# Expert stage of a hybrid encoder block: transposes gathered into long stretches, a third gather buffer and a second one-hot set

## Chip, core and metric

The kernel runs on one NeuronCore of a Trainium2 chip. The metric is the device time of one execution in microseconds (us), given as the median of the runs shown. A core has a matrix engine (TensorE, PE in the profile), a vector engine (DVE), a scalar engine (ACT), GpSimd (POOL) and SyncE (SP); the last two issue most of the DMAs. Matrix products land in PSUM, which has eight banks of 128 x 512 float32.

## The reference, cut to what matters

One encoder layer on 512 tokens of width 1024: attention and a state-space mixer, then a mixture of 16 experts in 4 groups, of which each token takes two. The change lies in the expert part alone. The reference computes every expert on every token and weighs it:

```
for e in range(N_EXPERTS):
    y_e = (jax.nn.silu(t @ w1[e]) * (t @ w3[e])) @ w2[e]
    out = out + combine[:, e:e + 1] * y_e
```

w1 and w3 are 1024 x 512, w2 is 512 x 1024, all float32: 6 MB for an expert, 96 MB for the 16.

## The kernel before

Each expert has 96 slots for its tokens. The 16 experts are taken in four **quads**: quad q holds the experts 4j + q, j = 0 to 3, one for each strip of 32 columns of the TensorE array. A **row block** r (0 to 2) of a quad is 128 rows: 32 slots of each of its four experts. For each of the 12 pairs (q, r) the kernel does this:

- **One-hot and indices.** `s_oh` writes on DVE which token sits in which slot (bf16, 128 x 512), `s_mm` multiplies it on TensorE (banks `pia`, `piq`) with the table `rc`, which holds token numbers and weights, and `s_ix` turns the result into indices.
- **Gather.** `gather` is an indirect DMA of GpSimd that fetches 128 tokens of 1024 float32 from `h2_d` into a gather buffer (`GS`). Row block (0, 0) comes without a gather.
- **Turn.** `t_mm` transposes the tokens on TensorE, four 128 x 128 blocks to a PSUM bank `pg`, two banks for a row block; `t_out` copies them to `TH`, on ACT (first half) and DVE (second).
- **Up.** `up_mm` multiplies with w1 (bank `pu`) and w3 (`pv`): eight jobs of four matmuls, each in a strip of 32 columns, that run side by side. `g_silu` and `g_mul` make the gated product in `s_buf`.
- **Turn again.** `s_t` transposes the product into one bank `ps`, and `s_out` copies it.
- **Down.** `down_mm` multiplies with w2 (bank `py`, two halves h, four k each), `y_ev` scales the result into `YS`.
- **Scatter.** An indirect DMA of GpSimd adds the 128 rows to `out`. Each scatter waits for the one before it, since both add to the same tensor.

The quads are interleaved in 12 phases, `u` (w1), `v` (w3) and `w` (w2): u0 v0 u1 w0 v1 u2 w1 v2 u3 w2 v3 w3. In quad 0, row block 0 goes through u and v first, then blocks 1 and 2. Each float32 matmul leaves two records in the trace, so that a job of up or down shows as eight. In w3 the order is row block by row block, so that block 0 needs the last weights of all, its k = 3, after a few jobs; the three last scatters then follow one another.

The **weights** come in 192 loads of 512 KB, 16 to a phase, issued by SP in the order of use. A load needs a free buffer of the pool "e". There are 35: 18 of their own, 3 that staged earlier weights, and 14 that come free as earlier tiles die, two from each call of `more` (tiles `EXm`, `EXx0`, `EXx1`, `EXr0`, `EXr1`, `EXu0`, `EXu1`). A buffer is free again when all row blocks have used it (`spent`).

The order on TensorE, ACT, DVE and GpSimd is laid down when the program is built: `Plan.run` is a list scheduler over jobs with costs, dependences, buffer pools and priorities (`prio`). Each engine then runs its list in that order.

Of the kernel before, what the change touches and what calls it, by code (L numbers as in the profile page):

```python
# [214 lines left out]
def tile_block(ctx: ExitStack, tc: tile.TileContext, x, norm_mix_w, w_in, b_gate, q_norm_w, k_norm_w,  # L215
# [19 lines left out]
    def bank(tag, nm):  # L235
        return psp.tile([P, 512], F32, tag=tag, name=nm, bufs=PSB[tag])
# [1349 lines left out]
    ohp = [cp.tile([P, NT, P], BF16, name="oh_%d" % i) for i in range(NR)]  # L1586

# [7 lines left out]
    def T_(q, r):  # L1595
        i = (q % 2) * NR + r
        return TH[i // 2][:, i % 2]

    def g_buf(R):
        return GS[0][:, R % NG, :]  # L1600

    def y_buf(r):
        return YS[r][:, :]
# [1 line left out]
    def s_buf(r):  # L1605
        return (YS[3][:, 0:512], YS[3][:, 512:1024], GS[1][:, 0, 0:512])[r]

    def sT_(r):
        return (GS[1][:, 0, 512:1024], GS[1][:, 1, 0:512], GS[1][:, 1, 512:1024])[r].rearrange(K4, k=4)

    def rooms():
        for t in TH + GS:
            t[:, 0]
        for t in YS:
            t[:, 0:512]


    def s_oh(q, r):
        V.tensor_tensor(ohp[r].rearrange("p t (j i) -> p t j i", j=4),
                        iota[:, r * RN:(r + 1) * RN].unsqueeze(1).unsqueeze(1).to_broadcast([P, NT, 4, RN]),  # L1620
                        slot.rearrange("p t (j q) -> p t j q", q=NQ)[:, :, :, q:q + 1].to_broadcast([P, NT, 4, RN]),
                        op=ALU.is_equal)

    def s_mm(nm, q, rs, n):
        t_["pi", nm] = bank("tp", "pi" + nm)
        for r in rs:
            for t in range(NT):
                T.matmul(t_["pi", nm][:, r * 18:r * 18 + n], lhsT=ohp[r][:, t, :], rhs=rc[:, t, q, 0:n], start=(t == 0),
                         stop=(t == NT - 1))

    def pi_(nm):
# [25 lines left out]
    def gather(g, i):  # L1657
        G.indirect_dma_start(g, None, h2_d, bass.IndirectOffsetOnAxis(ap=i, axis=0))

    def t_mm(q, r, kb):  # L1660
        g = g_buf(NR * q + r)
        pt = t_["pg", q, r, kb] = bank("tp", "pg%d_%d_%d" % (q, r, kb))
        for j in range(4):
            T.transpose(pt[:, j * P:(j + 1) * P], g[:, (kb * 4 + j) * P:(kb * 4 + j + 1) * P], ident)  # L1664

    def t_out(q, r, kb, src):
        o, i = T_(q, r)[:, kb * 4:kb * 4 + 4, :], src.rearrange(K4, k=4)
        if kb:
# [39 lines left out]
    def s_t(q, r):  # L1708
        t_["ps", q, r] = bank("tp", "ps%d_%d" % (q, r))
        for j in range(4):  # L1710
            T.transpose(t_["ps", q, r][:, j * P:(j + 1) * P], s_buf(r)[:, j * P:(j + 1) * P], ident)  # L1711

    def s_out(q, r):
        A.activation(sT_(r), t_["ps", q, r].rearrange(K4, k=4), AF.Copy)  # L1714
# [34 lines left out]
    jw, jT, jti, jsT, jy, jmul, jgx = {}, {}, {}, {}, {}, {}, {}  # L1749
    for x_, q in phases:  # L1750
        for kk in range(4):
            for j in range(4):
# [3 lines left out]
                    [j_rq] + ([last["e"]] if "e" in last else []), ["e"], prio=1000 + len(jw), lat=DLAT)  # L1756

    def sl_jobs(q):
        o = (0, at["u", 0] + 60, at["u", 1] - 90, at["u", 2] - 90)[q] or 700
        rs = list(range(NR))  # L1760
        oh = [job("dve", 0.6, lambda r=r: s_oh(q, r), [j_slot[t] for t in range(NT)] + (jti.get(q - 1, [])[:1]),
                  prio=o + (0 if r else 15) * (q == 0)) for r in rs]
# [23 lines left out]
    def t_jobs(q):
        for r in range(NR):
            o = (1900, at["v", 0] + 40 + 6 * r) [q] if q < 2 else at["w", q - 2] + 1 + r if r < 2 else at["v", q - 1] + 3
            jT[q, r] = []
            for kb in range(2):  # L1790
                tk = ["T"] * (kb == 0)
                if (q, r) == (0, 0):
                    k_, free = pgj[kb], ["sc"]
                else:
                    k_ = [job("pe", 0.55, lambda r=r, kb=kb: t_mm(q, r, kb), [jgx[q, r]] + jT[q, r], ["tp"],
                              ["G"] if kb else [], prio=o + r, duty=0.5)]
                    free = ["tp"]
                jT[q, r] = jT[q, r] + [job(
                    "dve" if kb else "act", 0.6 if kb else 0.48,
                    lambda r=r, kb=kb: t_out(q, r, kb, t_["pg", kb] if (q, r) == (0, 0) else t_["pg", q, r, kb]),  # L1800
                    k_ + [j_rooms], tk, free, prio=o - 1500)]

    def up_jobs(x_, q, prev, rs=tuple(range(NR))):
        o, tags = at[x_, q] + 30 * (q == 0 and rs[0] > 0), ("sc", "sc", "sc") if x_ == "v" else ("mm", "mm", "ac")
        nk = KD
        order_ = [(r, k) for k in range(nk) for r in rs]
        if (x_, q) == ("v", NQ - 1):
            order_.sort(key=lambda o_: o_ if o_[1] >= nk - 2 else (-1, o_[1]))
        for n, (r, k) in enumerate(order_):
            dep = [jw[x_, q, k // 2, j] for j in range(4)] + jT[q, r] + prev  # L1810
            end = (r, k % 2) == (NR - 1, 1)

            def f(r=r, k=k, end=end):
# [166 lines left out]
```

## Time and profile before

| | us |
|---|---|
| median of 3 runs | 670.3 (668.96 to 670.93) |
| the profiled execution, its own time | 669.12 |
| its span in the profile | 667.3 |
| TensorE busy in it | 645.5 |

The expert stage is the stretch from about 380 us to the end. "Busy" of TensorE counts any instruction in flight, so a full share says that it always had work, not that all of this work is needed. Load and landing times are those of the profile; a transfer's landing is the time at which its semaphore tells of it. Weights are moved by DMA queue q1, gathers and scatters by GpSimd's queue q0, and all of them by the same 16 DMA engines.

### The profile page before, as it was taken

To read this page: it belongs to the slowest core of one execution; us is meant where nothing else is said; L and a number is where in the kernel's file an instruction comes from. 1 tells how busy PE (TensorE), PEld (TensorE's weight loads), DVE (VectorE), ACT (ScalarE), POOL (GpSimd) and SP (SyncE) were. 2 spreads that over 40 slices of the span, in tenths; PEclk is the share of its full clock that TensorE was granted. 3 is DMA by queue.
4 is the path that set the end of the run, shared out by engine and by line. 5 is a ranking of instruction groups with operands and counts; after the bars stand their busy time and mean duration, and the time that the engine had idled before them with its cause. 6 is when DMAs were issued, how large, how long until landed. Compare 5 with 4: busy or idle time off the path is not lost. (4 is left out here: it accounts for less than half of the span.)

```text
span 667.3 us, 11451 instructions
## 1 busy us (share of the span) xinstructions
PE 645.5 (97%) x4636; PEld 394.4 (59%) x4637; DVE 324.3 (49%) x663; ACT 249.5 (37%) x450; POOL 83.5 (13%) x111
## 2 busy tenths in 40 slices
PE   7899999999999999999999899999999999999993
PEld 5788887777788888888877633333333333333320
DVE  5779968987698997466464851110110010001110
ACT  5535555777667778633444310101100210011010
POOL 4624100232000000000002110101020001000111
PEclk9999999999999999999999999999999999999998
DMA  8721733574221112698726878999999999999944
GB/s 288 194 76 37 187 78 81 139 210 127 65 64 32 32 33 64 205 362 306 293 83 216 313 256 323 409 407 409 401 359 383 408 408 352 383 408 399 358 102 65
DMA packets 79612, 155.37 MB, mean 233 GB/s; under 512 B 8568, under 2 KB 44932, under 8 KB 79556
## 3 DMA queue, kind: packets, MB, share of 16 engines
q1 hardware_dynamic: 70692, 131.79, 55.0%
q0 software_dynamic: 6800, 22.76, 12.8%
q8 instruction: 37, 0.61, 0.4%
q10 hardware_dynamic: 2064, 0.07, 0.2%
q14 instruction: 19, 0.16, 0.1%
HBM read 144.01 MB, written 10.58 MB: 232 GB/s over the span
## 5 line engine op out<-in xcount | busy, mean ns | idle before, releaser
L268 PE MATMUL b<-hTh,wc_hi 128*128 128x512 f32 x208 | 84.5, 406 | 0.0
L270 PE MATMUL b<-hTh,wc_lo 128*128 128x512 f32 x208 | 81.4, 391 | 0.0
L269 PE MATMUL b<-hTl,wc_hi 128*128 128x512 f32 x208 | 81.3, 391 | 0.0
L1687 PE MATMUL py<-w,GS 128*32 128x512 f32 x564 | 64.4, 593 | 0.1
L1679 PE MATMUL pu<-u,TH 128*32 128x512 f32 x528 | 63.3, 593 | 0.0
L1679 PE MATMUL pv<-v,TH 128*32 128x512 f32 x372 | 58.9, 593 | 0.0
L1850 DVE TENSOR_SCALAR YS<-py,ti 128x512 f32<-128x512 f32 x12 | 9.0, 751 | 89.9 <-PE py L1687 89.6
L1669 DVE COPY TH<-pg 128x512 f32<-128x512 f32 x12 | 8.3, 691 | 79.8 <-PE pg L1664 79.7
L663 ACT ACTIVATE wc_hi<-wc_r 128x1024 fp32r<-128x1024 f32 x34 | 36.0, 1059 | 29.3 <-PE b L269 22.2
L1714 ACT ACTIVATE GS<-ps 128x512 f32<-128x512 f32 x12 | 7.0, 601 | 103.3 <-PE ps L1711 103.3
L667 DVE TENSOR_TENSOR wc_lo<-wc_r,wc_hi 128x1024 fp32r<-128x1024 f32 x34 | 41.5, 1222 | 7.5 <-ACT wc_hi L663 7.4
L268 PEld LDWEIGHTS b<-hTh,wc_hi 128*128 128x128 f32 x208 | 39.0, 188 | 9.7 <-issue 1.5
L270 PEld LDWEIGHTS b<-hTh,wc_lo 128*128 128x128 f32 x208 | 39.1, 188 | 8.7
L269 PEld LDWEIGHTS b<-hTl,wc_hi 128*128 128x128 f32 x208 | 39.1, 188 | 7.1
L1687 PEld LDWEIGHTS py<-w,GS 128*32 128x32 f32 x564 | 18.3, 110 | 38.3 <-issue 35.1
L1679 PEld LDWEIGHTS pu<-u,TH 128*32 128x32 f32 x528 | 17.9, 110 | 38.3 <-issue 37.1
L1717 POOL DMA_INDIRECT out_dram<-YS,sx x12 | 18.7, 1561 | 142.2 <-DVE YS L1850 68.1
L1679 PEld LDWEIGHTS pv<-v,TH 128*32 128x32 f32 x372 | 15.4, 110 | 29.9 <-issue 29.2
L1679 PE MATMUL pv<-EXr,TH 128*32 128x512 f32 x96 | 32.7, 595 | 0.0
L1852 ACT ACTIVATE YS<-py,ti 128x512 f32<-128x512 f32 x12 | 8.3, 688 | 58.6 <-PE py L1687 43.4
L1706 DVE TENSOR_TENSOR YS<-YS,pv 128x512 f32<-128x512 f32 x8 | 5.5, 688 | 46.0 <-PE pv L1679 46.0
L1679 PE MATMUL pv<-EXx,TH 128*32 128x512 f32 x120 | 26.8, 593 | 0.0
(359 smaller groups left out, 1420.2 us busy)
## 6 DMA issues: line engine op xcount, KB each, us to landing
w<-in_w_dram SPq DMA_DIRECT2D x47, 512.0 KB, 12.4
u<-in_w_dram SPq DMA_DIRECT2D x44, 512.0 KB, 8.7
v<-in_w_dram SPq DMA_DIRECT2D x31, 512.0 KB, 10.2
wc_r<-in_w_in_dram SPq DMA_DIRECT2D x26, 512.0 KB, 5.1
EXx<-in_w_dram SPq DMA_DIRECT2D x20, 512.0 KB, 11.3
EXr<-in_w_dram SPq DMA_DIRECT2D x20, 512.0 KB, 12.6
EXu<-in_w_dram SPq DMA_DIRECT2D x20, 512.0 KB, 10.8
EXm<-in_w_dram SPq DMA_DIRECT2D x10, 512.0 KB, 11.4
```

Of the source, the lines that this page charges most:

```text
L268: T.matmul(ps, lhsT=lh, rhs=rh, start=first, stop=False)
L269: T.matmul(ps, lhsT=lh, rhs=rl, start=False, stop=False)
L270: T.matmul(ps, lhsT=ll, rhs=rh, start=False, stop=last)
L663: A.activation(t_["w", i][0], t_["raw", i], AF.Copy)
L667: V.tensor_tensor(l_, t_.pop(("raw", i)), h_.bitcast(F32), op=ALU.subtract)
L1669: V.tensor_copy(o, i)
L1679: T.matmul(t_["p", x_, q, r][js, :], lhsT=T_(q, r)[:, k, js], rhs=t_["raw", x_, q, k // 2, j][:, k % 2, :], start=k == 0, stop=k == KD - 1)
L1687: T.matmul(t_["p", h, q, r][js, :], lhsT=sT_(r)[:, k, js], rhs=t_["raw", "w", q, k, j].rearrange("p a n -> p (a n)")[:, int(h) * 512:(int( ...
L1714: A.activation(sT_(r), t_["ps", q, r].rearrange(K4, k=4), AF.Copy)
L1717: G.indirect_dma_start(out, bass.IndirectOffsetOnAxis(ap=sx[q][:, r:r + 1], axis=0), y_buf(r), None, compute_op=ALU.add)
L1850: V.tensor_scalar(o, i, w_, None, op0=ALU.mult)
L1852: A.activation(o, i, AF.Copy, scale=w_)
```

## The change

The transposes of tokens and of gated products are no longer jobs of one bank each. A job of `turn_jobs` makes up to five banks one after the other (`turn`, banks `ptt` and `pts`), and the copies follow, on ACT and DVE in turn. Each row block r has its own gather buffer: the third is half of a new tile `GX`. The other half of `GX` holds the one-hot set of the odd quads. `GX` takes the place of `EXm`, so the pool "e" has two buffers fewer. The core of the diff:

```diff
-NG = 2
+NG = 3
...
-    def g_buf(R):
-        return GS[0][:, R % NG, :]
+    GX = Late(h8, "GX", F32, "p (a n) -> p a n", a=2)
+
+    def g_buf(r):
+        return GS[0][:, r, :] if r < 2 else GX[:, 0, :]
+
+    def oh_(q, r):
+
+        if q % 2 == 0:
+            return ohp[r]
+        return GX[:, 1, r * 256:(r + 1) * 256].bitcast(BF16).rearrange("p (t s) -> p t s", t=NT)
...
+    def turn(g, tag):
+
+        pt = t_["pt", g] = bank(tag, "pt%s%d_%d" % (g[0], g[1], g[2] * 2 + g[3]))
+        src = g_buf(g[2])[:, g[3] * 512:(g[3] + 1) * 512] if g[0] == "t" else s_buf(g[2])
         for j in range(4):
...
+    def turned(g, on_v):
+        o, i = T_(g[1], g[2])[:, g[3] * 4:g[3] * 4 + 4, :] if g[0] == "t" else sT_(g[2]), t_["pt", g].rearrange(K4, k=4)
+        if on_v:
             V.tensor_copy(o, i)
         else:
             A.activation(o, i, AF.Copy)
...
-    more(h8, "EXm", [j_rooms])
...
-        o = (0, at["u", 0] + 60, at["u", 1] - 90, at["u", 2] - 90)[q] or 700
+        o = (700, at["u", 0] + 8, at["v", 0] + 38, at["v", 0] + 39)[q]
...
+    def turn_jobs(prio, tags, groups):
+
+        dep, take, free = [], list(tags), []
+        for x_, q, r, kb in groups:
+            if x_ == "t":
+                dep.append(jgx[q, r])
+                take += ["T"] * (kb == 0)
+                free += ["G"] * kb
+            else:
+                dep.append(jm[q, r])
+                free.append("s")
+        k_ = job("pe", 0.44 * len(groups) + 0.2, lambda: [turn(g, tag) for g, tag in zip(groups, tags)], dep, take, free, prio=prio, duty=0.5)
+        for i, (g, tag) in enumerate(zip(groups, tags)):
+            j_ = job("dve" if i % 2 else "act", 0.65, lambda g=g, i=i: turned(g, i % 2), [k_], ["sT"] * (g[0] == "s"), [tag], prio=prio - 1500)
+            if g[0] == "t":
+                jT.setdefault(g[1:3], []).append(j_)
+            else:
+                jsT[g[1:3]] = j_
...
+    u_, v_ = [[at[x_, q] for q in range(NQ)] for x_ in "uv"]
     prev, jsc = [], []
-    for rs in ((0,), (1, 2)):
-        for x_ in "uv":
-            prev = up_jobs(x_, 0, prev, rs)
+    for x_ in "uv":
+        prev = up_jobs(x_, 0, prev, (0,))
+    turn_jobs(v_[0] + 7, ("tp", "tp", "sc", "sc"), tg(0, 1) + tg(0, 2))
+    for x_ in "uv":
+        prev = up_jobs(x_, 0, prev, (1, 2))
+    turn_jobs(v_[0] + 34, ("tp", "tp", "mm", "mm"), tg(1, 0) + tg(1, 1))
+    turn_jobs(v_[0] + 40, ("tp", "tp", "mm"), tg(1, 2) + sg_(0, 0))
     for x_, q in phases[2:]:
-        if x_ in "uv":
+        if x_ == "u":
             prev = up_jobs(x_, q, prev)
+            s_ = sg_(q - 1, 0, 1, 2)[q == 1:]
+            if q < NQ - 1:
+                turn_jobs(u_[q] + 6, ("tp", "tp", "sc", "sc", "sc")[q == 1:], s_ + tg(q + 1, 0))
+                turn_jobs(u_[q] + 14, ("tp", "tp", "sc", "sc"), tg(q + 1, 1) + tg(q + 1, 2))
+            else:
+                turn_jobs(u_[q] + 6, ("tp", "tp", "sc"), s_)
+        elif x_ == "v":
+            prev = up_jobs(x_, q, prev)
+            for r in range(NR) if q == NQ - 1 else ():
+                turn_jobs(v_[q], ("tp",), sg_(q, r))
```

**DVE, just ahead of the expert stage.** `oh_147` to `oh_149` are the one-hot set, `cw` and `lp` the routing weights that go into `rc`; `TH` takes quad 0's first turned tokens, `ix` its gather indices. Before, behind the three rows of quad 0's one-hot set:

```order
L1496 TENSOR_REDUCE lp_3258<-cw 128x4
L1580 COPY cnt<-plt 128x16
L1497 RECIPROCAL lp_3258<-lp_3258 128x4
L1883 COPY tab<-slot 128x16x4
L1877 TENSOR_SCALAR nxf<-cnt 128x16
L1498 TENSOR_TENSOR cw<-cw,lp_3258 128x64
L1669 COPY TH_3661<-pg_3682 128x512
```

After, the same place:

```order
L1496 TENSOR_REDUCE lp_3258<-cw 128x4
L1580 COPY cnt<-plt 128x16
L1627 TENSOR_TENSOR GX<-cst,slot 128x512
L1678 COPY TH_3661<-pg_3681 128x512
L1646 TENSOR_SCALAR ix_3795<-pia 128x2
L1903 TENSOR_SCALAR nxf<-cnt 128x16
L1909 COPY tab<-slot 128x16x4
L1647 TENSOR_TENSOR ix_3795<-ix_3795,pia 128x2
L1497 RECIPROCAL lp_3258<-lp_3258 128x4
L1627 TENSOR_TENSOR GX<-cst,slot 128x512
L1498 TENSOR_TENSOR cw<-cw,lp_3258 128x64
L1627 TENSOR_TENSOR GX<-cst,slot 128x512
```

Three rows of 128 x 512 into `GX`, quad 1's one-hot set, now stand ahead of most steps that complete the table `rc`, which TensorE's first full product with the one-hot set (`piq`) reads; before, quad 1's set was written into `oh_147` to `oh_149` behind that product.

**PE, phase u1.** `ps` and `pts` are transposes of gated products, `pg` and `ptt` of tokens, `pu` the product with w1. Before, the phase begins so:

```order
L1664 MATMUL pg_1_0_4195<-cst,GS_3664 128x128 x4
L1679 MATMUL pu_0_4201<-EXu_3824,TH_3662 32x512
L1679 MATMUL pu_0_4201<-EXr_3877,TH_3662 32x512 x2
L1679 MATMUL pu_0_4201<-u_0_3_3996,TH_3662 32x512
L1711 MATMUL ps_0_4207<-cst,YS_3669 128x128 x4
L1664 MATMUL pg_1_1_4214<-cst,GS_3664 128x128 x4
L1711 MATMUL ps_1_4222<-cst,YS_3669 128x128 x4
L1679 MATMUL pu_1_4228<-EXu_3824,TH_3663 32x512
L1679 MATMUL pu_1_4228<-EXr_3877,TH_3663 32x512 x2
L1679 MATMUL pu_1_4228<-u_0_3_3996,TH_3663 32x512
L1711 MATMUL ps_2_4235<-cst,GS_3665 128x128 x4
```

After:

```order
L1692 MATMUL pu_0_4256<-u_1_2_4036,TH_3662 32x512
L1692 MATMUL pu_0_4256<-u_1_3_4046,TH_3662 32x512
L1673 MATMUL pts_2_4293<-cst,YS_3670 128x128 x4
L1673 MATMUL pts_4_4298<-cst,GS_3665 128x128 x4
L1673 MATMUL ptt_0_4303<-cst,GS_3664 128x128 x4
L1673 MATMUL ptt_1_4308<-cst,GS_3664 128x128 x4
L1692 MATMUL pu_1_4264<-u_1_0_4020,TH_3663 32x512
L1692 MATMUL pu_1_4264<-u_1_1_4030,TH_3663 32x512
```

What stood as bank, four matmuls, three banks, four matmuls, then three more banks is now one stretch of four banks after seven jobs of u1. Over the expert stage 34 banks are turned in both programs, in 23 stretches before and in 11 after. In the opening, the v jobs of quad 0's row block 0 were cut by stretches of one, two and one bank; now its eight jobs run through, and one stretch of four banks follows. The first `piq` stands behind four jobs of u0 in place of three.

**SP, where the loads first wait for TensorE.** `EX..` and `u_..` are buffers; the row of `u` is the first that waits for a buffer to be spent. Before:

```order
L1722 DMA EXx_3575<-in_w_dram 128x1024 x2
L1722 DMA EXm<-in_w_dram 128x1024 x2
L1722 DMA EXx_3731<-in_w_dram 128x1024 x2
L1722 DMA EXr_3764<-in_w_dram 128x1024 x2
L1722 DMA EXu_3796<-in_w_dram 128x1024 x2
L1722 DMA EXu_3824<-in_w_dram 128x1024 x2
L1722 DMA EXr_3877<-in_w_dram 128x1024 x2
L1722 DMA u_0_3_3996<-in_w_dram 128x1024
L1722 DMA u_1_0_4002<-in_w_dram 128x1024
```

After:

```order
L1727 DMA EXx_3575<-in_w_dram 128x1024 x2
L1727 DMA EXx_3729<-in_w_dram 128x1024 x2
L1727 DMA EXr_3762<-in_w_dram 128x1024 x2
L1727 DMA EXu_3792<-in_w_dram 128x1024 x2
L1727 DMA EXu_3815<-in_w_dram 128x1024 x2
L1727 DMA EXr_3876<-in_w_dram 128x1024 x2
L1727 DMA u_0_1_3998<-in_w_dram 128x1024
L1727 DMA u_0_2_4004<-in_w_dram 128x1024
```

The two loads into `EXm` are gone, all others have moved up, and the first load that waits for TensorE is the 34th of the 192 in place of the 36th. On GpSimd the order of gathers also changes: all 11 now stand ahead of the first scatter, where two stood behind scatters.

## Rows read from the trace of the kernel before

**Rows 1.** Page, part 1: busy us, share of the span, instructions.
```profile
PE 645.5 (97%) x4636; PEld 394.4 (59%) x4637; DVE 324.3 (49%) x663; ACT 249.5 (37%) x450; POOL 83.5 (13%) x111
```

**Rows 2.** Chain of waits in order of time, its first long piece: start, us, what.
```profile
637.75 4.49 PE py L1687 x37
```

**Rows 3.** Timeline of SP, which issues the expert loads: start us, us, instruction.
```profile
381.39 0.93 SPq L1722 DMA_DIRECT2D EXr<-in_w_dram  x2
402.68 7.67 SPq L1722 DMA_DIRECT2D u<-in_w_dram  x10
...
612.59 0.33 SPq L1722 DMA_DIRECT2D w<-in_w_dram  x1
619.77 0.33 SPq L1722 DMA_DIRECT2D w<-in_w_dram  x1
625.22 0.33 SPq L1722 DMA_DIRECT2D w<-in_w_dram  x1
```

**Rows 4.** DMA issues at 612.59, 619.77, 625.22: KB each, us to landing.
```profile
w<-in_w_dram SPq DMA_DIRECT2D x1, 512.0 KB, 12.6
w<-in_w_dram SPq DMA_DIRECT2D x1, 512.0 KB, 12.9
w<-in_w_dram SPq DMA_DIRECT2D x1, 512.0 KB, 12.5
```

**Rows 5.** Waits of SP's queue, 381 to 415 us: total us, times, longest.
```profile
SPq L1722 <- PE pu L1679: 22.1, 3, 19.5
```

**Rows 6.** Waits of PE, 399 to 645 us: total us, times, longest.
```profile
PE ps L1711 <- ACT GS L1714: 0.9, 3, 0.3
```

**Rows 7.** Busy time by stretch: length, engines' busy us, granted clock, DMA share, GB/s.
```profile
592.00:602.00 10.00, 10.00 (x100) 3.09 (x96) 0.00 (x0) 0.47 (x1) 0.00 (x0) 1.00 1.03 410
402.70:632.70 230.00, 228.65 (x2088) 74.15 (x2084) 24.58 (x53) 23.01 (x40) 19.27 (x15) 1.00 1.02 389
655.00:661.00 6.00, 0.97 (x6) 0.06 (x1) 0.75 (x1) 0.00 (x0) 1.55 (x1) 0.99 0.44 66
661.00:667.00 6.00, 0.00 (x0) 0.00 (x0) 0.00 (x0) 0.00 (x0) 0.00 (x0) 0.50 0.32 63
```

**Rows 8.** Timeline of PE around three short stretches of transposes in quad 0's w.
```profile
456.27 1.92 PE L1687 MATMUL py<-w,GS 128*32 128x512 f32 x16
459.15 1.92 PE L1687 MATMUL py<-w,GS 128*32 128x512 f32 x16
461.59 1.06 PE L1687 MATMUL py<-w,GS 128*32 128x512 f32 x8
```

**Rows 9.** Timeline of PE, opening of the expert stage.
```profile
380.58 2.78 PE L1679 MATMUL pu<-u,TH 128*32 128x512 f32 x24
383.80 0.46 PE L1628 MATMUL piq<-rc,oh 128*128 128x18 bf16 x12 [0.44 <-DVE rc L1505]
...
399.06 13.92 PE L1679 MATMUL pu<-u,TH 128*32 128x512 f32 x128
```

**Rows 10.** Timeline of DVE just before the expert stage.
```profile
378.29 1.89 DVE L1619 TENSOR_TENSOR oh<-cst,slot 128x512 bf16<-128x512 f32 x3
...
383.30 0.45 DVE L1505 COPY rc<-mk 128x64 bf16<-128x64 bf16 x1
```

**Rows 11.** Timeline of POOL: fourth and fifth gather, last scatter of quad 2.
```profile
397.66 0.94 POOL L1658 DMA_INDIRECT GS<-h_d,ix  x1 [2.48 <-PE pg L1664]
425.38 0.94 POOL L1658 DMA_INDIRECT GS<-h_d,ix  x1 [26.78 <-PE pg L1664]
...
632.71 1.55 POOL L1717 DMA_INDIRECT out_dram<-YS,sx  x1 [9.15 <-DMA out_dram<-YS,sx]
```

**Rows 12.** GpSimd's DMA queue, 439.5-444.5, 615.5-621.5, 632.7-637.7 us: packets, MB, share of 16 engines.
```profile
q0 software_dynamic: 144, 0.52, 26.4%
q0 software_dynamic: 144, 0.52, 43.8%
q0 software_dynamic: 84, 0.34, 41.1%
```

More of the change, by code (lines that the diff above doesn't have):

```diff
@@ L1585, in tile_block @@
     w2v = w2[0].rearrange("e (p k) f -> e p k f", p=P)
-    ohp = [cp.tile([P, NT, P], BF16, name="oh_%d" % i) for i in range(NR)]
+    ohp = [cp.tile([P, NT, P], BF16, name="oh_%d" % r) for r in range(NR)]
     TH = [Late(h8, "TH%d" % i, F32, "p (a k s) -> p a k s", a=2, k=KD) for i in range(NR)]
@@ L1611, in rooms @@
     def rooms():
-        for t in TH + GS:
+        for t in TH + GS + [GX]:
             t[:, 0]
@@ L1618, in s_oh @@
     def s_oh(q, r):
-        V.tensor_tensor(ohp[r].rearrange("p t (j i) -> p t j i", j=4),
+        V.tensor_tensor(oh_(q, r).rearrange("p t (j i) -> p t j i", j=4),
                         iota[:, r * RN:(r + 1) * RN].unsqueeze(1).unsqueeze(1).to_broadcast([P, NT, 4, RN]),
@@ L1627, in s_mm @@
             for t in range(NT):
-                T.matmul(t_["pi", nm][:, r * 18:r * 18 + n], lhsT=ohp[r][:, t, :], rhs=rc[:, t, q, 0:n], start=(t == 0),
+                T.matmul(t_["pi", nm][:, r * 18:r * 18 + n], lhsT=oh_(q, r)[:, t, :], rhs=rc[:, t, q, 0:n], start=(t == 0),
                          stop=(t == NT - 1))
@@ L1658, in gather @@
         G.indirect_dma_start(g, None, h2_d, bass.IndirectOffsetOnAxis(ap=i, axis=0))
-    def t_mm(q, r, kb):
-        g = g_buf(NR * q + r)
-        pt = t_["pg", q, r, kb] = bank("tp", "pg%d_%d_%d" % (q, r, kb))
+    def turn(g, tag):
+        pt = t_["pt", g] = bank(tag, "pt%s%d_%d" % (g[0], g[1], g[2] * 2 + g[3]))
+        src = g_buf(g[2])[:, g[3] * 512:(g[3] + 1) * 512] if g[0] == "t" else s_buf(g[2])
         for j in range(4):
[L1664 to L1668, printed above, removed]
+            T.transpose(pt[:, j * P:(j + 1) * P], src[:, j * P:(j + 1) * P], ident)
+    def turned(g, on_v):
+        o, i = T_(g[1], g[2])[:, g[3] * 4:g[3] * 4 + 4, :] if g[0] == "t" else sT_(g[2]), t_["pt", g].rearrange(K4, k=4)
+        if on_v:
             V.tensor_copy(o, i)
@@ L1671, in t_out, with first_out @@
             A.activation(o, i, AF.Copy)
+    def first_out(kb):
+        t_["pt", ("t", 0, 0, kb)] = t_["pg", kb]
+        turned(("t", 0, 0, kb), kb)
     def up_mm(x_, q, r, k, tag):
@@ L1706, in g_mul @@
         V.tensor_tensor(s_, s_, by_k(t_["p", "v", q, r]), op=ALU.mult)
[L1708 to L1714, printed above, removed]
     def scatter(q, r):
@@ L1748, in tile_block @@
     at = {ph: 2000 + 100 * i for i, ph in enumerate(phases)}
-    jw, jT, jti, jsT, jy, jmul, jgx = {}, {}, {}, {}, {}, {}, {}
+    jw, jT, jti, jsT, jy, jmul, jgx, jm, jg_ = {}, {}, {}, {}, {}, {}, {}, {}, []
     for x_, q in phases:
@@ L1758, in sl_jobs @@
     def sl_jobs(q):
-        o = (0, at["u", 0] + 60, at["u", 1] - 90, at["u", 2] - 90)[q] or 700
+        o = (700, at["u", 0] + 8, at["v", 0] + 38, at["v", 0] + 39)[q]
         rs = list(range(NR))
-        oh = [job("dve", 0.6, lambda r=r: s_oh(q, r), [j_slot[t] for t in range(NT)] + (jti.get(q - 1, [])[:1]),
+        oh = [job("dve", 0.6, lambda r=r: s_oh(q, r), [j_slot[t] for t in range(NT)] + [j_rooms] * (q % 2) + (jti.get(q - 2, [])[:1]),
                   prio=o + (0 if r else 15) * (q == 0)) for r in rs]
@@ L1766, in sl_jobs @@
         nm = "q%d" % q
-        k_ = job("pe", 0.5, lambda: s_mm(nm, q, rs, 18), oh + [j_w5] + ([jx] if q == 0 else []), ["tp"], prio=o + 5, duty=0.1)
+        k_ = job("pe", 0.5, lambda: s_mm(nm, q, rs, 18), oh + [j_w5] + ([jx] if q == 0 else []), ["tp"], prio=o + 5 * (q == 0), duty=0.1)
         j_ = k_
@@ L1777, in sl_jobs @@
         for i in range(NR + 6):
-            j_ = job("dve", 0.09, lambda i=i: step(i), [j_], free=["tp"] if i == NR + 5 else [], prio=o + 6)
+            j_ = job("dve", 0.09, lambda i=i: step(i), [j_], free=["tp"] if i == NR + 5 else [], prio=o + 6 * (q == 0))
         jti[q] = [k_, j_]
@@ L1781, in sl_jobs @@
             if (q, r) != (0, 0):
-                k_ = job("pool", 1.03, lambda r=r: gather(g_buf(NR * q + r), ix[q][:, r:r + 1]), [jx, j_rooms] + j_h2,
+                k_ = job("pool", 1.03, lambda r=r: gather(g_buf(r), ix[q][:, r:r + 1]), [jx, j_rooms] + j_h2 + jg_[-1:],
                          ["G"], prio=o + r)
+                jg_.append(k_)
                 jgx[q, r] = job("dma", 1.3, lambda: None, [k_], prio=-500, lat=6.0)
[L1786 to L1801, printed above, removed]
@@ L1803, in up_jobs, with tg, sg_ @@
+    def tg(q, r):
+        return [("t", q, r, 0), ("t", q, r, 1)]
+    def sg_(q, *rs):
+        return [("s", q, r, 0) for r in rs]
+    jT[0, 0] = [job("dve" if kb else "act", 0.65, lambda kb=kb: first_out(kb), pgj[kb] + [j_rooms], ["T"] * (kb == 0), ["sc"], prio=400) for kb in range(2)]
     def up_jobs(x_, q, prev, rs=tuple(range(NR))):
@@ L1823, in up_jobs @@
                 else:
-                    k_ = job("dve", 0.6, lambda r=r: g_mul(q, r), prev + [jmul[q, r]], [], [tags[r]], prio=p_)
-                    k_ = job("pe", 0.64, lambda r=r: s_t(q, r), [k_], ["tp"], ["s"], prio=o + 130 + r if q < NQ - 1 else o, duty=0.5)
-                    jsT[q, r] = job("act", 0.48, lambda r=r: s_out(q, r), [k_], ["sT"], ["tp"], prio=p_)
+                    jm[q, r] = job("dve", 0.6, lambda r=r: g_mul(q, r), prev + [jmul[q, r]], [], [tags[r]], prio=p_)
         return prev
```

1 line of the change is left out of this document (removed).

## Prediction

> **What bounds the kernel now.** I read the page first. TensorE is busy 645.5 us of the span, 97% [rows 1], and in the expert stage 228.65 of 230 us [rows 7]. That invites the reading that every microsecond taken from TensorE is a microsecond off the kernel. The chain of waits speaks against it: followed back from the end, it begins with TensorE work at 637.75 us [rows 2], in the middle of w3, at the k = 3 job of row block 0. SP issued the last weight load at 625.22 [rows 3], and it landed 12.5 us later [rows 4], at 637.7. So the last part of the kernel, 667.3 - 637.75 = 29.6 us, starts when the last weights land: the rest of row block 0 and the three scatters in turn.
>
> The next view is the load stream. Where loads run alone the 16 DMA engines move 410 GB/s with a share of 1.03 [rows 7]; a load of 512 KB, 0.524 MB, is 1.28 us of them. From 402.7 to 632.7 the share is 1.02, with gathers and scatters in between [rows 7]. Ahead of that SP waited 19.5 us for TensorE to give a buffer back [rows 5]: nothing is issued from 381.39 until 402.68 [rows 3]. So the weights' end is the time of the restart plus everything that the DMA engines do between: 157 loads (192 less the 35 buffers), seven of the 11 gathers (the fourth is issued at 397.66, the fifth at 425.38 [rows 11]), and scatters. TensorE and the loads arrive at 637.7 nearly together, but the loads have the last word.
>
> **The change part by part.** The sum is made for the landing of the last weights, 637.7 before.
>
> *Shorter turns on TensorE.* From 456.27 to 459.15, 2.88 us, lie 16 records and two banks; from 459.15 to 461.59, 2.44 us, 16 records and one bank [rows 8]. The second bank costs 0.44. The 16 records are four steps; a step is (1.92 - 0.59)/3 = 0.44 (0.59 is one matmul), 1.77 in all. So one bank alone costs 0.67, of which 0.23 is going over and back. From the restart on, ten stretches fewer remain (17 before the last three, against seven): 2.3 us. The waits for copies inside the stretches of gated products, 0.9 us [rows 6], go too. TensorE reaches the end of w2 some 3.2 us sooner, plus what the opening gives. For the landing this is worth nothing in itself.
>
> *Opening.* `piq` waited 0.44 us for `rc`, the last step of which starts at 383.30 [rows 9, 10]. Three one-hot writes of 1.89/3 = 0.63 us [rows 10] now stand ahead of that step, so `rc` is ready about 1.8 us later, near 385.5; TensorE, with four jobs of 0.86 us from 380.58 [rows 9], could take it at 384.0 and waits 1.5. Then come `piq` itself (0.4), four jobs (3.4), the second product with the one-hots (0.5), eight jobs (6.9) and a stretch of four banks (0.23 + 4 x 0.44 = 2.0): u of row blocks 1 and 2 starts near 398.7, against 399.06 [rows 9]. The restart comes 0.3 us sooner. Were `rc` not late, it would be 1.8 sooner; were the copies of that stretch waited for in full, 0.7 later. I keep 0.3, since DVE's rows stand in that order.
>
> *Two buffers fewer.* The DMA engines stood nearly idle ahead of the restart because every buffer was full. Two loads less fit there and move behind it: 2 x 1.28 = +2.6 us. Nothing hides them, since no slack is left behind the restart. The Trainium skill, "DMA: Bandwidth & Descriptors", section "Specifications", puts one core's HBM limit at about 358 GB/s; by that a load would take an estimated 1.46 us, and the whole sum below would be 0.4 us larger. The trace's 410 GB/s [rows 7] differs and decides.
>
> *Third gather buffer.* Quad 1's first gather can go as soon as its indices are there, the other two when the first stretch has emptied their buffers, near 397.5 and 398.7. All three are then ahead of the restarted loads, one more than before, and so in idle time. A gather takes 26.4% of 5 us, 1.3 us of all DMA engines [rows 12]: -1.3. If the third is late and meets the loads, 0. I take -1.3, because the restart's first packets follow the issue at 402.68 [rows 3] by over 1 us.
>
> *Scatters.* A scatter takes 43.8% of 6 us, 2.6 us of the DMA engines [rows 12], twice a gather. Quad 2's last one was issued at 632.71 [rows 11], while the last four loads were under way. The load issued at 619.77 landed at 632.7, the last at 637.7 [rows 3, 4]: four loads in 5.1 us, 1.28 each, so this scatter cost them nothing. The four loads before, landing from 612.59 + 12.6 = 625.2 to 632.7, took 7.5 us with one scatter among them, 2.4 more. With TensorE 3.2 + 0.3 us ahead at the end of w2, the three scatters, each waiting for the one before, are issued 3.5 us sooner, the last near 629.2, and it is served before the last weights: +2.4. Lower bound: by its queue's share it had already 2.05 of its 2.63 us before 637.7 [rows 12], which leaves +0.6. I take 2.4, as landings, not shares, release TensorE.
>
> *No price.* Copies alternating between ACT and DVE, the new banks' tags and the moved index products act on TensorE alone, which now waits for loads by several us at the end of w3; without that cover they would cost what they delay. SP's loads are issued some 10 us ahead of landing [rows 4], so that waits for one of 33 buffers by a us or two starve nothing.
>
> **Sum.** -0.3 + 2.6 - 1.3 + 2.4 = +3.4 us on the last landing, near 641.1. The 29.6 us behind it stay. The profiled execution of 669.1 becomes 672.5. It lies 1.2 us under the median of 670.3, within the runs shown; on the median the sum gives 673.7.
>
> **The rivals.**
>
> *TensorE sets the end (faster).* If the loads had slack, the 3.5 us come off: 666.8. For it: TensorE's 97% [rows 1]. Against: the chain's start at the last landing. It decides only if the last weights land before about 634.
>
> *The loads hold their time (no change).* If the last scatter of quad 2 costs 0.6 in place of 2.4, and the restart comes a us earlier, the sum is +0.6: 670.9. For it: the share of 41.1% [rows 12]. Against: the 1.28 us per load to the end.
>
> *The clock falls while TensorE waits (slower still).* TensorE is ready for its last loads 3.5 us sooner and gets them 3.4 later, some 7 us of waiting, broken by one job of 0.86 for each load that lands. Behind the last matmul, at about 656.0, the granted clock stays at full until nearly 661 and is 0.50, the 1.2 GHz level, after it [rows 7]. By the Trainium skill, "TensorE: Matmul & The Clock Gate", section "HAM oscillation — how this bites in real kernels", a TensorE that waits for a DMA between bursts starts the next burst at half clock; no row here shows such a restart. The 4.49 us of TensorE work at the head of the chain [rows 2] would take up to twice as long: half of that, 2.2 us more, gives 675.9. Against: the landing loads keep giving it work.
>
> **How the numbers follow.** A difference under 0.3%, 2.0 us, can't be told from no change here. Forecast, 60%: 673.7, itself from 672.2 (restart 1.8 us sooner) to 675.0 (third gather in the loads' way). Clock, 13%: 675.9, at most 678.2. Loads hold, 19%: 670.9. TensorE sets the end, 8%: 666.8. The range goes from 669.5 to 677.0: below, the loads hold and the restart is 1.8 us sooner, which sums to +0.1, 670.4, less 0.9 for the spread of the runs; above, it lies between the clock's two prices. Faster is the last case, 0.08; no change the third and the forecast's lower edge, 0.21; slower the rest, 0.71.
>
> **What would show it.** Right: the first load that waits for TensorE is issued near 402.4; `piq` waits over 1 us for `rc`; five gathers are issued ahead of the restart; quad 2's last scatter is issued near 629; the last weights land near 641; and TensorE, without waits before, has some 6 us of waits for `w` in w3. The chain again begins at that landing. Wrong: a last landing at or before 638, or a chain that runs through TensorE's work in w2. A granted clock under 1.00 between 632 and 650 is the third rival. The prediction fails if the scatter doesn't delay the last loads, or if the opening gives TensorE back more than I let it.

## The result, and the profile after

| | us |
|---|---|
| changed kernel, median of 6 runs | 674.88 (674.34 to 675.41) |
| kernel before beside it, median of 6 | 670.15 (668.96 to 670.93) |
| ratio, 95% interval | 1.0069 (1.0057 to 1.0081) |
| profiled execution after, its own time / its span | 675.01 / 673.2 |

The change costs 4.7 us. The forecast was 673.7, 3.4 us more than before: slower, for the reason given, but a little more so.

Busy time by engine (the page's first part), to be read against [rows 1]:

```profile
PE 649.0 (96%) x4635; PEld 398.4 (59%) x4637; DVE 325.4 (48%) x666; ACT 248.9 (37%) x447; POOL 84.6 (13%) x111
```

TensorE is busy 3.5 us more, although it turns the same banks in fewer stretches; "busy" says nothing of where the saving went. The chain of waits does. Its first long piece [rows 2]:

```profile
643.17 4.49 PE py L1700 x37
```

The chain again begins at the last landing, now 5.42 us later, and behind it lie 673.2 - 643.17 = 30.0 us against 29.6. So nearly the whole loss (the two spans differ by 5.9) is in the landing of the last weights. SP's timeline shows that it did not arise at the restart (start, us, instruction, to be read against [rows 3]):

```profile
382.71 0.90 SPq L1727 DMA_DIRECT2D EXr<-in_w_dram  x2
402.71 1.36 SPq L1727 DMA_DIRECT2D u<-in_w_dram  x3
...
629.32 1.60 SPq L1727 DMA_DIRECT2D EXr<-in_w_dram  x2
```

The restart is at 402.71 against 402.68; the last load is issued near 630.6 against 625.22. TensorE, in contrast, is early: quad 2's scatters mark the end of w2 (timeline of POOL, to be read against [rows 11]; the first line is quad 2's first scatter in the trace before).

```profile
611.32 1.55 POOL L1717 DMA_INDIRECT out_dram<-YS,sx  x1 [43.44 <-DVE YS L1850]
...
606.25 1.55 POOL L1722 DMA_INDIRECT out_dram<-YS,sx  x1 [41.30 <-DVE YS L1862]
616.86 1.55 POOL L1722 DMA_INDIRECT out_dram<-YS,sx  x1 [9.07 <-DMA out_dram<-YS,sx]
627.64 1.55 POOL L1722 DMA_INDIRECT out_dram<-YS,sx  x1 [9.23 <-DMA out_dram<-YS,sx]
649.19 1.55 POOL L1722 DMA_INDIRECT out_dram<-YS,sx  x1 [20.00 <-DVE YS L1862]
```

Quad 2's first is issued at 606.25 against 611.32, 5.1 us sooner, and its last at 627.64 against 632.71. TensorE then waits for weights in w3, where it had no such wait before [rows 6] (waits of PE, 399 to 645 us):

```profile
PE py L1700 <- DMA EXx<-in_w_dram: 3.0, 3, 2.5
PE py L1700 <- DMA w<-in_w_dram: 0.4, 2, 0.2
PE py L1700 <- DMA EXr<-in_w_dram: 0.2, 1, 0.2
```

Windows (length, busy us of PE, PEld, DVE, ACT and POOL, granted clock, DMA share, GB/s), against [rows 7]:

```profile
402.70:642.70 240.00, 236.26 (x2126) 77.44 (x2118) 25.43 (x54) 23.52 (x38) 19.68 (x15) 1.00 1.02 383
...
632.00:650.00 18.00, 14.28 (x80) 3.07 (x82) 0.75 (x1) 1.29 (x2) 0.81 (x1) 1.00 0.46 154
379.70:383.10 3.40, 3.40 (x24) 2.05 (x27) 3.16 (x13) 0.60 (x1) 0.00 (x0) 0.50 1.03 419
```

The DMA engines are as full as before from the restart to the end, for 240 us in place of 234.5. The clock stayed full in w3, but it was 0.50, the 1.2 GHz level, for 3.4 us at the start of the expert stage, where the trace before has full clock:

```profile
379.70:383.10 3.40, 3.40 (x39) 1.52 (x38) 3.40 (x22) 0.51 (x1) 0.56 (x1) 1.00 1.02 393
```

TensorE thus came to `piq` at 385.81 without the wait that I had forecast (timelines of PE and DVE):

```profile
381.43 4.45 PE L1692 MATMUL pu<-u,TH 128*32 128x512 f32 x32
385.81 0.46 PE L1636 MATMUL piq<-rc,oh 128*128 128x18 bf16 x12
```

```profile
385.33 0.24 DVE L1505 COPY rc<-mk 128x64 bf16<-128x64 bf16 x1
```

`rc` is complete at 385.57, as late as forecast (385.5), but half a clock has taken TensorE's time in its place.

One thing more shows behind the restart: what each queue moved in the 12 us from it on (packets, MB, share of 16 engines), first before (402.68 to 414.68), then, in two lines, after (402.71 to 414.71).

```profile
q1 hardware_dynamic: 1088, 4.00, 90.5%
...
q1 hardware_dynamic: 1006, 3.69, 85.9%
q0 software_dynamic: 118, 0.42, 9.7%
```

Before, no gather was moving at that point. After, the fourth and fifth gathers, issued at 398.53 and 399.78 and landed 4.4 and 5.2 us later, still moved 0.42 MB, and the loads 0.31 MB less than before, 0.8 us at 410 GB/s.

### The profile page after: what moved, and what is told of

Its sections match the earlier page's. It is cut to its first block, busy times and chain, and to the rows that moved or that the text cites. A ratio compares the mean times of both kernels' runs of the same rounds, so it can differ in the third digit from the quotient of the medians.

```text
span 673.2 us, 11454 instructions
## 1 busy us (share of the span) xinstructions
PE 649.0 (96%) x4635; PEld 398.4 (59%) x4637; DVE 325.4 (48%) x666; ACT 248.9 (37%) x447; POOL 84.6 (13%) x111
## 5 line engine op out<-in xcount | busy, mean ns | idle before, releaser
L1692 PE MATMUL pu<-u,TH 128*32 128x512 f32 x600 | 69.7, 599 | 0.0
L1700 PE MATMUL py<-w,GS 128*32 128x512 f32 x456 | 65.8, 592 | 0.4 <-DMA w<-in_w_dram 0.4
L1692 PEld LDWEIGHTS pu<-u,TH 128*32 128x32 f32 x600 | 19.5, 111 | 40.5 <-issue 38.1
L1680 ACT ACTIVATE GS<-pts 128x512 f32<-128x512 f32 x9 | 5.4, 597 | 94.1 <-PE pts L1673 94.1
L1700 PE MATMUL py<-EXx,GS 128*32 128x512 f32 x144 | 34.5, 593 | 3.1 <-DMA EXx<-in_w_dram 3.0
L1692 PEld LDWEIGHTS pv<-v,TH 128*32 128x32 f32 x456 | 16.3, 110 | 30.4 <-issue 29.5
L1700 PE MATMUL py<-EXr,GS 128*32 128x512 f32 x96 | 27.3, 593 | 0.4 <-DMA EXr<-in_w_dram 0.2
```

The source lines that it names most:

```text
L1692: T.matmul(t_["p", x_, q, r][js, :], lhsT=T_(q, r)[:, k, js], rhs=t_["raw", x_, q, k // 2, j][:, k % 2, :], start=k == 0, stop=k == KD - 1)
L1700: T.matmul(t_["p", h, q, r][js, :], lhsT=sT_(r)[:, k, js], rhs=t_["raw", "w", q, k, j].rearrange("p a n -> p (a n)")[:, int(h) * 512:(int( ...
```

## The experiments

All times are medians; "before" is the kernel before beside them on the same chip. The last columns come from the one profiled execution of each: the start of TensorE's last `plt` product of the routing (L1459, just ahead of the expert stage), the first load that waits for TensorE (restart), the time between these two (opening), the end of the last weights' packets, the stretch from the restart to it, and the rest of the span.

| run | median | before | ratio (95%) | plt | restart | opening | weights end | stretch | rest |
| --- | --- | --- | --- | --- | --- | --- | --- | --- | --- |
| before | | | | 377.56 | 402.68 | 25.1 | 637.23 | 234.5 | 30.1 |
| after | 674.88 | 670.15 | 1.0069 (1.0057-1.0081) | 377.69 | 402.71 | 25.0 | 642.71 | 240.0 | 30.5 |
| e1 33 buffers | 677.74 | 670.68 | 1.0103 (1.0084-1.0123) | 378.05 | 403.90 | 25.9 | 643.82 | 239.9 | 32.2 |
| e2 stretches | 673.23 | 670.68 | 1.0050 (1.0030-1.0071) | 378.26 | 402.26 | 24.0 | 640.24 | 238.0 | 30.1 |
| e3 stretches, 33 | 676.30 | 670.68 | 1.0082 (1.0060-1.0104) | 378.54 | 403.54 | 25.0 | 645.61 | 242.1 | 30.3 |
| e4 after, late scatter | 675.66 | 670.68 | 1.0076 (1.0056-1.0095) | 380.80 | 406.54 | 25.7 | 643.98 | 237.4 | 30.1 |
| e5 the same, in place | 672.83 | 670.26 | 1.0037 (1.0023-1.0051) | 378.43 | 404.15 | 25.7 | 641.78 | 237.6 | 30.3 |
| e6 after, rc first | 675.03 | 670.26 | 1.0060 (1.0040-1.0081) | 378.79 | 403.82 | 25.0 | 643.39 | 239.6 | 30.4 |
| e7 stretches, late scatter | 671.31 | 670.26 | 1.0016 (1.0004-1.0028) | 378.60 | 402.62 | 24.0 | 639.97 | 237.4 | 30.6 |
| e8 e7 and early restart | 667.76 | 670.26 | 0.9963 (0.9952-0.9974) | 378.16 | 399.18 | 21.0 | 635.38 | 236.2 | 29.9 |
| e9 e1, late scatter | 673.99 | 670.67 | 1.0056 (1.0042-1.0069) | 379.14 | 405.29 | 26.2 | 642.60 | 237.3 | 30.1 |
| e10 before, late scatter | 670.03 | 670.67 | 0.9994 (0.9982-1.0006) | 378.39 | 403.58 | 25.2 | 638.05 | 234.5 | 30.2 |
| e11 e8, scatter early | 672.65 | 670.67 | 1.0036 (1.0019-1.0052) | 379.06 | 400.78 | 21.7 | 639.41 | 238.6 | 31.5 |

One profile stands for each kernel. In the stretch, after and e6, which move the same loads, gathers and scatters, differ by 0.4 us, e4 and e5 by 0.2. The start of `plt` differs by up to 1.6 us (e4 apart), although no edit touches TensorE's work ahead of it: DVE's 21st instruction (L573) already starts at 24.45 us before, at 24.59 after and at 24.94 to 26.02 in the others. So a later restart is not all due to an edit; the opening leaves this out. The sums below go by medians and use the profiles for the place.

**e1: two buffers alone.**

```diff
-    more(h8, "EXm", [j_rooms])
```

> The kernel before, with EXm taken out of the pool e: 33 buffers, nothing else changed. If the landing of the last weights sets the end, two loads move from idle time behind the restart: the last landing 2.6 us later, time 670.15 + 2.6 = 672.8. If TensorE sets the end, the two buffers are worth nothing: within 0.5 us of the kernel before, and its last landing has no later work hanging on it. If the loads have slack that takes up part of it, between 0.5 and 2.

Measured: 677.74, 7.1 us slower than before, far over the 2.6. TensorE as the bound is out. The restart came 1.2 later, 0.5 of it there at `plt` and 0.7 in the opening, where the clock was low. The stretch is 5.4 longer, 2.6 of it the two loads. The rest of the span is 2.1 longer, and here the clock fell (timeline of PE, then windows):

```profile
639.49 1.04 PE L1687 MATMUL py<-EXx,GS 128*32 128x512 f32 x2 [0.40 <-DMA EXx<-in_w_dram]
643.02 2.28 PE L1687 MATMUL py<-EXr,GS 128*32 128x512 f32 x3 [2.49 <-DMA EXr<-in_w_dram]
```

```profile
632.00:640.00 8.00, 7.59 (x54) 2.11 (x52) 1.09 (x2) 1.79 (x3) 1.55 (x1) 1.00 1.03 381
642.00:648.00 6.00, 4.97 (x21) 1.86 (x25) 0.00 (x0) 0.69 (x1) 0.00 (x0) 0.50 0.10 37
```

That is the third rival, in another kernel: after a wait of 2.49 us TensorE ran the head of the chain at 1.2 GHz. What remains of the stretch, some 2.8 us, e9 tells.

**e2 and e3: the stretches alone, and with 33 buffers.** The third gather buffer and the second one-hot set are taken back, and with them DVE's order at the opening; in e3 `EXm` is gone as well.

```diff
-        return GS[0][:, r, :] if r < 2 else GX[:, 0, :]
+        return GS[0][:, R % NG, :]
...
-        return GX[:, 1, r * 256:(r + 1) * 256].bitcast(BF16).rearrange("p (t s) -> p t s", t=NT)
...
+    more(h8, "EXm", [j_rooms])
```

> The stretches of transposes alone: 35 buffers, two gather buffers, one one-hot set, DVE's order at the opening as before. Loads theory: restart up to 1.8 us sooner since the table rc is on time, quad 2's last scatter some 4 us sooner and so in front of the last weights (+2.4): between +0.6 and +2.4, 670.8 to 672.6, although TensorE does less. TensorE theory: the 3.2 us of going over and waiting come off, and up to 1.8 in the opening: 665 to 667.

> The stretches alone with 33 buffers, so the changed kernel without its third gather buffer and second one-hot set. Loads theory: 2.6 above the stretches with 35 buffers. Against the changed kernel (674.9) it lacks the fifth gather ahead of the restart (+1.3) and has the table rc in time (0 to -1.5): 674.7 to 676.2. Rival, that the fifth gather runs into the restarted loads and is what made the steady part of the lag 2 us larger than forecast: 1 to 2 below the changed kernel, 673 to 674.

Measured: e2 673.23, 2.55 us slower than before. The part of the change that takes work from TensorE makes the kernel slower by itself; its rival had 665 to 667. e3 is 676.30, 3.1 over e2: the price of two buffers on this side, where 2.6 was forecast. And the changed kernel, 674.88, is 1.4 under e3: the third gather buffer, with the second one-hot set and DVE's order, gives 1.4 back against a kernel that has the stretches already, and the rival that the fifth gather does harm falls, which had e3 at 673 to 674. e3's six runs lie between 674.35 and 677.63, so neither difference is good to better than 1.5 to 2 us.

**e4 and e5: quad 2's last scatter held back.** Two small operations of GpSimd read one column of the third-last weight load, multiply it by zero and add it to the scatter's indices, so that the scatter is issued when that load has landed. In e4 the result has a tile of its own; in e5 it lies in a one-hot buffer that is free by then.

The core of e5's edit:

```diff
+    def gate(q, r):
+        g = ohp[r][:, 0, 0:2].bitcast(I32)
+        G.tensor_scalar(g, t_["raw", "w", 3, 3, 1][:, 0, 0:1], 0.0, None, op0=ALU.mult)
+        G.tensor_tensor(g, g, sx[q][:, r:r + 1], op=ALU.add)
...
```

> The changed kernel with one thing moved: quad 2's last scatter takes its indices through two small GpSimd operations that read the third-last weight load, so that it goes out only when that load has landed. By the forecast's term of 2.4 for this scatter the last weights land 2.4 us sooner, near 640.8, and the time is 672.5. By its lower bound of 0.6: 674.3. If the scatter has nothing to do with it: 674.9.

> The changed kernel with quad 2's last scatter held back until the third-last load has landed, as in the run before, but its indices are kept in a column of a one-hot buffer that is no longer used, so that no tile in front of the expert stage moves to another address. In that run the stretch from the restart to the last weights' bytes was 237.4 us against 240.0 of the changed kernel, but all that lies before the restart took 3.8 us longer. If that came from the added tile, the scatter is now seen alone: 674.9 - 2.6 = 672.3. If a later start goes with the late scatter: 675.7 again.

Measured: e4 675.66, at first sight a miss. But its stretch is 2.6 shorter, and everything ahead of it 3.8 longer: 3.1 of that is there at `plt`, most of it with the added tile (last section), and 0.7 lies in the opening, as in e5. e5, without the tile, is 672.83, 2.05 under the changed kernel, with a stretch 2.4 shorter. The scatter in front of the last weights costs 2.05; the forecast took 2.4 from between 0.6 and 2.4.

**e6: the table `rc` first.** The one-hot sets of the odd quads wait on DVE until `rc` is done.

```diff
-        oh = [job("dve", 0.6, lambda r=r: s_oh(q, r), [j_slot[t] for t in range(NT)] + [j_rooms] * (q % 2) + (jti.get(q - 2, [])[:1]),
+        oh = [job("dve", 0.6, lambda r=r: s_oh(q, r), [j_slot[t] for t in range(NT)] + [j_rooms, j_w5] * (q % 2) + (jti.get(q - 2, [])[:1]),
```

> The changed kernel with quad 1's one-hot set written only behind the table rc on DVE; all else as in it. By the forecast's opening, where the late table costs TensorE 1.5 us, the restart comes 1.5 us sooner: 673.4. By the trace of the changed kernel, where TensorE ran at half clock from 379.7 to 383.1 and came to piq at 385.8, 0.24 us after the table was done, the order of DVE costs nothing: 674.9.

Measured: 675.03, no gain. DVE's order at the opening is worth nothing as long as the clock falls there, as it did in this profile too.

**e7: stretches with the late scatter.** The gate of e5 in e2.

> The stretches alone (35 buffers) with quad 2's last scatter held back until the third-last load has landed. Loads theory: the scatter no longer stands in front of the last weights, 2.5 us off the 673.2 of the stretches alone: 670.7, and TensorE waits some 0.6 us for loads in w3 in place of 3.1. If the scatter's place doesn't matter: 673.2.

Measured: 671.31, 1.9 under e2 where 2.5 was expected; TensorE's waits for `w` are 1.4 in place of 3.1. Of e2's 2.55 us, 1.9 are the scatter; the other 0.6 (e7 is 1.05 over the kernel before beside it) remain. For them the profiles have a candidate that no run separates: in e2 the third and fourth gathers go out at 398.07 and 399.32, behind the stretch of four banks, in place of 394.23 and 397.66, and are still moving when the loads restart. In the 12 us from the restart on the loads move 3.56 MB in e2 and 3.37 in e7, against 4.00 before and 4.06 in e10: 1.1 to 1.7 us at 410 GB/s, against 1.1 that e2 and e7 gain in the opening.

**e8 and e11: an early restart, with and without the late scatter.** In e8 (built on e7) and e11 (on e2) the first stretch, and u of row blocks 1 and 2 behind it, move ahead of the last four v jobs of row block 0, so that all three row blocks are through with the first buffers sooner; the index products of quads 2 and 3 are kept behind.

```diff
-    for x_ in "uv":
-        prev = up_jobs(x_, 0, prev, (0,))
+    prev = up_jobs("u", 0, prev, (0,))
+    prev = up_jobs("v", 0, prev, (0,), range(4))
     turn_jobs(v_[0] + 7, ("tp", "tp", "sc", "sc"), tg(0, 1) + tg(0, 2))
-    for x_ in "uv":
-        prev = up_jobs(x_, 0, prev, (1, 2))
+    prev = up_jobs("u", 0, prev, (1, 2))
+    for q in (2, 3):
+        sl_jobs(q, prev)
+    prev = up_jobs("v", 0, prev, (0,), range(4, KD))
+    prev = up_jobs("v", 0, prev, (1, 2))
```

> As the run with the stretches and the late scatter, and in the opening the first stretch of four banks stands behind four of the eight v jobs of row block 0, u of row blocks 1 and 2 follows at once and the other four v jobs come behind it. The first buffers of quad 0 are then free some 3.6 us sooner, near 398.7. If the loads set the end, they stop doing so: TensorE, which without waits could come to the last weights of row block 0 near 634.5, sets it, and the time is 667.5. If the landing of the last weights depends on something else than the restart and the DMA engines' work: 670.7 as without it.

> The run with the early restart (667.8) without the late scatter: stretches, 35 buffers, u of row blocks 1 and 2 after four v jobs. There the last weights landed near 635.4 and TensorE waited 0.7 us. With the scatter, issued near 627, in front of the last weights again they land up to 2.4 us later, and TensorE has nothing else to do: 669.5 to 670.2. If TensorE set the end in that run with slack to spare in the loads: 667.8.

Measured: e8 667.76, faster than the kernel before by 2.5 us and than the changed one by about 7. The waits of SP's queue (382 to 412 us) and the timelines of PE and POOL in w3 show it:

```profile
SPq L1733 <- PE pu L1688: 17.1, 4, 14.1
```

```profile
633.34 1.05 PE L1696 MATMUL py<-w,GS 128*32 128x512 f32 x2 [0.23 <-DMA w<-in_w_dram]
634.61 1.04 PE L1696 MATMUL py<-w,GS 128*32 128x512 f32 x2 [0.23 <-DMA w<-in_w_dram]
635.86 4.50 PE L1696 MATMUL py<-w,GS 128*32 128x512 f32 x40 [0.21 <-SPq L1983]
```

```profile
633.38 0.26 POOL L1721 TENSOR_SCALAR oh<-w 128x1 int32<-128x1 f32 x1 [15.20 <-DMA w<-in_w_dram]
...
634.50 1.61 POOL L1726 DMA_INDIRECT out_dram<-YS,oh  x1 [0.59 <-POOL oh L1722]
641.89 1.58 POOL L1728 DMA_INDIRECT out_dram<-YS,sx  x1 [5.77 <-DVE YS L1872]
```

The longest wait ahead of the restart is 14.1 us against 19.1 in the changed kernel, the TensorE work that headed the chain in the changed kernel begins at 635.86, and the scatter lies in the rest of the span without delaying the next. TensorE waits 0.2 us from matmul to matmul, so it and the last weights come nearly together. That the stretches have a part in this gain is not shown: no run has the early restart and the late scatter without them.

e11 is 672.65, 4.9 over e8, twice what I expected. In its profile the restart is 1.6 later, 0.9 of it there at `plt` and 0.7 in the opening, with the clock low (0.54, against 1.00 in e8); the stretch is 2.4 longer, the scatter; and the rest is 1.6 longer, with the clock at 0.50 for a while after a wait of 2.46 us (windows, e11):

```profile
380.00:383.00 3.00, 3.00 (x16) 3.00 (x17) 2.32 (x9) 0.60 (x1) 0.00 (x0) 0.54 0.98 341
632.00:639.00 7.00, 3.96 (x16) 0.71 (x15) 0.00 (x0) 0.60 (x1) 0.00 (x0) 1.00 0.68 195
640.00:643.00 3.00, 3.00 (x16) 0.58 (x13) 0.00 (x0) 0.69 (x1) 0.00 (x0) 0.50 0.00 0
```

So a scatter in front of the last weights costs 2.4 in the stretch, and 1.6 more here (2.1 in e1) where the clock is low after the wait that it makes.

**e9 and e10: the late scatter in e1 and in the kernel before.**

> The kernel before with 33 buffers (677.7 in its first run, 7 above the kernel before) and quad 2's last scatter held back until the third-last load has landed. If the 7 us are 2.6 for two loads behind the restart, 1.2 for the clock that fell ahead of the stage, 2.4 for the scatter, in front of which the last weights no longer are, and the rest for the clock that fell after TensorE's wait at the last weights: the scatter's 2.4 go and with them part or all of the last term, 673.6 to 675.3. If two buffers cost 7 us in another way: 677.7 again.

> The kernel before with only quad 2's last scatter held back. There the scatter was issued too late to delay the last weights by more than a part of it, and TensorE, which has no transposes to spare, comes to them nearly when they land. So by the forecast's reading nothing is gained: 669.8 to 670.5. If the loads alone set the end and the scatter cost them its full 2.4: 668.

Measured: e9 673.99, 3.75 under e1; its stretch is 2.6 shorter and the low clock in w3 is gone. e10 670.03: no difference from before. The same scatter, at the same place in the program, costs nothing in the kernel before and 2.6 us of the stretch as soon as two loads more stand behind the restart: what counts is the order in time of the last weights and the scatter. In e1 TensorE was not early, the weights were late.

## Why the prediction came out

*Bound.* Right. The chain begins at the last landing in both kernels, and less work on TensorE alone (e2) made the kernel slower.

*Opening, -0.3.* Measured 0: the restart moved by +0.03 and the opening from 25.1 to 25.0 us, and with `rc` first (e6) it is 25.0 too. `rc` was as late as forecast, but the wait of over 1 us that I had named as a sign did not appear, since the clock had slowed TensorE by about as much. I had left the clock out of the opening. Where `rc` came as in the kernel before and the clock stayed full (e2, e7), the opening took 24.0, 1.1 less than before; the forecast had 1.8 for that.

*Two buffers, +2.6.* Right in kind: 3.1 measured (e3 against e2), 4.0 by e9 against e10, in whose profiles the restart is 1.7 later too, 0.75 of it there at `plt`. Two loads of 1.28 account for 2.6. Alone in the kernel before (e1) the buffers cost 7.1, for they put the last weights behind the scatter even without an early TensorE, and the clock fell: the terms of the sum do not stand for themselves. The Trainium skill, "DMA: Bandwidth & Descriptors", section "Specifications", whose 358 GB/s limit I had weighed, is not borne out: where loads ran alone after the change they moved 408 GB/s (592 to 602 us).

*Third gather, -1.3.* The term that was mis-sized. Against e3 it measures -1.4, but the forecast had it against the kernel before. Against that one the fifth gather no longer runs at 425 us, but it and the fourth ran into the restarted loads, and of the 1.3 us 0.8 went back (3.69 MB of loads against 4.00): about -0.5 is left. The forecast had named this case, "If the third is late and meets the loads, 0", with its edge of 675.0. It kept -1.3 with the two gathers issued near 397.5 and 398.7; they went out at 398.53 and 399.78, and landed at 402.9 and 405.0.

*Last scatter, +2.4.* The sum's decisive term, measured 2.05 (e5) and 1.9 (e7). It was issued at 627.64, with 629 forecast, since TensorE was 5.1 us ahead and not 3.5: the shorter turns gave more than the 3.2 forecast, and the first scatters of quads 0, 1 and 2 are 1.4, 3.1 and 5.1 us sooner.

*Sum.* The medians go from before to e2, e3 and the changed kernel by +2.55, +3.1 and -1.4. That these add up is no test, as each begins where the one ahead ends; they make 4.2 from one median of the kernel before (670.68) and 4.7 from the other (670.15). The forecast's terms, with 0 for the opening and -0.5 for the third gather, make 0 + 2.6 - 0.5 + 2.4 = 4.5, or 4.2 with the scatter at 2.05. So of the 1.3 by which the forecast fell short, most is the gather term (0.8) and the opening (0.3). The mechanism is right: the last weights land later, by two loads and a scatter.

*Signs.* Five gathers were issued ahead of the restart, as said, but the last two had not landed. The last weights landed at 643.1 in place of 641. TensorE's waits for loads in w3 were 3.6 in place of 6: each of the last loads that landed gave it a single matmul of 1.04 us, where four run side by side in 0.86, and I had counted too little of this.

*Rivals.* TensorE as the bound and loads that hold their time are out. The falling clock did not appear in the changed kernel's profile (1.00 from 632 to 650), though TensorE waited (timeline of PE):

```profile
636.94 2.19 PE L1700 MATMUL py<-EXx,GS 128*32 128x512 f32 x4 [2.54 <-DMA EXx<-in_w_dram]
```

It did fall in w3 of four others: in e1 and e11, after waits of 2.49 and 2.46 us, where it added 2.1 and 1.6 to the rest of the span; and in e2 and e6, where waits of 1.70 and 1.17 us, and one of 2.38, stand at it, and the rest stayed at 30.1 and 30.4 (windows of e2, then e6):

```profile
636.00:640.00 4.00, 3.10 (x5) 0.54 (x6) 0.00 (x0) 0.00 (x0) 0.00 (x0) 0.59 0.63 258
...
636.00:640.00 4.00, 2.74 (x4) 0.36 (x4) 0.00 (x0) 0.00 (x0) 0.00 (x0) 0.60 1.00 363
```

So such waits can have it or not, and that the changed kernel's runs were spared it is known from one profile only. The Trainium skill, "TensorE: Matmul & The Clock Gate", section "HAM oscillation — how this bites in real kernels", describes a kernel in which a TensorE that waits for a DMA between bursts starts the next one at half clock; e1, e2, e6 and e11 show such a fall, the changed kernel does not.

## What to carry to other kernels

Where loads and the matrix engine reach the end together, work taken from the engine is worth nothing until the loads are relieved by as much; here the kernel became faster only with an earlier restart of the loads and a late scatter beside the stretches (e8, 667.76), and what each of the three gives there alone is in part open. A buffer given up is a load moved from idle to saturated time. And when one engine gets faster, look at what it triggers on a shared resource, and when: a scatter issued 5 us sooner took its 2 us from the very transfer that everything waited for, and gathers meant for idle time ran into the loads behind it.

## What the hardware showed unexpectedly

*An 8-byte tile.* With e4's added tile of two columns (8 bytes a partition, made ahead of the other tiles of the expert stage) the projections' 128 x 512 products, far in front of it in time, became slower (groups of PE by line, 130 to 330 us; busy us, mean ns). The changed kernel:

```profile
L268 PE MATMUL b<-hTh,wc_hi 128*128 128x512 f32 x109 | 44.6, 409 | 0.0
L270 PE MATMUL b<-hTh,wc_lo 128*128 128x512 f32 x110 | 43.1, 391 | 0.0
```

e4:

```profile
L268 PE MATMUL b<-hTh,wc_hi 128*128 128x512 f32 x111 | 45.8, 413 | 0.0
L270 PE MATMUL b<-hTh,wc_lo 128*128 128x512 f32 x111 | 43.8, 395 | 0.0
```

4 ns in 391, 1%. From the same DVE instruction (L614, at 61 to 62 us) to `plt` e4 takes 318.9 us, the changed kernel and e5 316.3: 2.6 us. e5 has 409 and 391 again. That the cause is other addresses of the tiles is only argued from these two runs; no other offset was tried.

*The clock ahead of the expert stage.* In 7 of the 13 profiles TensorE's clock was at 1.2 GHz for about 3 us, beginning between 379 and 382 us (after, e1, e3, e4, e5, e6, e11), in 6 not (before, e2, e7 to e10), with the same TensorE instructions, and the same waits of 1.1 and 0.6 us, in front of it. The opening is 0.7 to 1.0 us longer with it (e1 against before, e3 against e2, e11 against e8). It follows neither the buffers (e9 has 33 and kept its clock, e11 has 35 and lost it) nor the stretches; what decides it stays open.
